# Folding a residual gate vector into the output weights of a transformer layer's merge stage

## The chip, the cores and the metric

The kernel runs on one core of one Trainium2 chip. The metric is device time in microseconds (us) of one execution; the time of a kernel is the median of its runs. The core has five engines with a queue of instructions each. TensorE (PE) multiplies matrices out of SBUF into PSUM; VectorE (DVE), ScalarE (ACT) and GpSimd (POOL) do elementwise work; the queue of SyncE (SP) issues nearly all the DMAs. Within one queue the order is fixed at compile time: an instruction that waits for another engine holds up everything behind it in its own queue.

## The reference, cut to what matters

One layer over 2048 latent tokens of width 1024. The stage that matters merges two branches, projects the result with `w_out`, and adds it to the residual stream `x` under a per-channel gate `g1` that comes from the conditioning vector:

```python
def branch_merge(attn_o, gm_o, ga_logit, gb_logit, w_br_attn, w_br_gm, w_out):
    y = jax.nn.sigmoid(ga_logit) * (attn_o @ w_br_attn) + jax.nn.sigmoid(gb_logit) * (gm_o @ w_br_gm)
    return y @ w_out
...
x = x + g1 * branch_merge(attn_x, gm_x, ga_x, gb_x, w_br_attn[l], w_br_gm[l], w_out[l])
h2 = modulate(x, norm2_g[l], sh2, sc2)
x = x + g2 * sq_relu_mlp(h2, w_ff1[l], w_ff2[l])
```

`g1` has one value for each of the 1024 output channels, the same for all tokens. So `g1 * (y @ w_out)` equals `y @ (w_out * g1)`, with `g1` multiplied into the columns of `w_out`.

## The kernel before, in words

**Number format.** Every large product is computed from two parts of each operand. `split` (L150) makes them: ACT casts the operand to a high part (L153), and POOL or DVE subtracts that from the operand to get the low part (L157). `mm3` (L184) then issues three matmuls for one product: high by high (L186), high by low (L187), low by high (L188).

**The order of stages.** First the projections, then attention, then `merge` (L1402), then the feed-forward network (`ffn`, L1973). `merge` runs over 4 blocks `b` of 512 tokens. Each block has two phases.

*Branch phase*, 8 steps `m`, one for each 128 channels of `y`. A step's program order is:

1. SP issues the loads for step n + 2 (`load`, L1417): raw branch weights and gates.
2. `cast(n + 1)` (L1421): the branch weights of the next step are split, for branch "g" and then for branch "a". ACT casts; the low part is made by DVE for the first three steps of the kernel (n = 0, 1, 2) and by POOL after that.
3. 24 matmuls on PE: 12 for branch "g", 12 for branch "a", each group into a PSUM bank of its own. The first low-part weights are needed by the third matmul of the step.
4. DVE multiplies each bank with its gate (L1466, twice), adds the two (L1469); then `y` is split: ACT casts, DVE subtracts.
5. In block 0 only, one step of `load_w_out` (L1325): it fetches the next 128 rows of `w_out` and splits the present ones, 128x1024 elements; ACT casts, DVE subtracts. After the 8 steps the 8 pairs in `self.wo` stay in SBUF for all four blocks.

Block 0 has two extras. After step 2 the softmax sums of the last attention unit are multiplied on PE and copied out by ACT (L2369). After step 4 DVE takes their reciprocal (`inverse`, L2382), and SP waits for it.

*Output phase*, 4 tiles `tt` of 128 tokens with 2 halves of 512 channels each: 24 matmuls into one bank (`outer`, L1495), then a step of side work (preparing the inputs of the next block, or in block 3 the first operands of the feed-forward network, `h_first`, L1579), then the bank is multiplied with the gate vector `g1b` into a scratch tile `part` (L1518), and `part` is added to the tile of `x` (L1519). A finished tile is stored, and ACT sums its squares (`stored`, L1429) for the next normalisation.

`g1b` (128x1024, the gate in every partition, already halved for the form of the sigmoid that is used) is finished during attention, before `merge` begins.

**What sets the order.** `merge` puts its whole range of instructions into `self.pins`, and `order` (L2063) ties every pinned instruction to the one before it on its engine. In this stage, then, each engine runs in exactly the order in which the Python code emits. The feed-forward network is not pinned; a planner at compile time orders its instructions by the readiness it works out.

Of the kernel before, what the change touches and what calls it, by code (L numbers as in the profile page):

```python
# [13 lines left out]
ALU = mybir.AluOpType  # L14
# [58 lines left out]
class Kern:  # L73
# [1251 lines left out]
    def load_w_out(self):  # L1325
        nc = self.nc
        self.wo = []

        def fetch(k):
            st = self.sb("wo", [D])  # L1330
            nc.sync.dma_start(st, self.I["w_out"][0, k * P : (k + 1) * P, :])
            return st

        ahead = fetch(0)
        yield
        for k in range(KC):
            st = ahead
            if k + 1 < KC:
                ahead = fetch(k + 1)
            h, l = self.sb("wo", [D], F32R), self.sb("wo", [D], F32R)  # L1340
            self.split(st, h, l, lo_eng="dve")
            self.wo.append((h, l))
            yield
# [58 lines left out]
    def merge(self, first, start, last, ops, w1):  # L1402
        nc = self.nc
        for _ in start:
            pass
        self.close("mid", "base")
        self.open("early")
        self.open("late", side="right")
        for tag, shape in (("md", [TB]), ("js", [HK]), ("gt", [TB])):
            self.sb(tag, shape)  # L1410
        begin = self.here()
        steps = [(b, m) for b in range(NB) for m in range(KC)]
        raws, gts, ws = {}, {}, {}
        w_out = self.load_w_out()
        mod = self.mod_part(lambda: self.sb("md", [TB]), ("sh2", "sc2"), True)

        def load(n, tag="gt"):  # L1417
            raws[n] = self.br_raw(steps[n][1])
            gts[n] = self.gate_in(*steps[n], tag)

        def cast(n, lo_eng):  # L1421
            ws[n] = self.br_weights(raws.pop(n), lo_eng)

        def x_row(b, tt):
            xt = self.sb("xt", [D])
            nc.sync.dma_start(xt, self.x_block(b)[tt * P : (tt + 1) * P, :])
            return xt

        def stored(b, tt, xt):  # L1429
            nc.sync.dma_start(self.x1_d[b][tt * P : (tt + 1) * P, :], xt)  # L1430
            junk = self.sb("jk", [D], mybir.dt.bfloat16)
            col = b * TT + tt
            nc.scalar.activation(
                junk, xt, AF.Square, accum_out=self.ss2[:, col : col + 1]
            )

        load(0, "gx")
        load(1)
        cast(0, "dve")
        last.leave(self.sb("raw", [TB]))  # L1440
        next(w_out)
        inp = first
        for b in range(NB):
            y = []
            for m in range(KC):
                n = b * KC + m
                if n + 2 < len(steps):
                    load(n + 2)
                if n + 1 < len(steps):
                    cast(n + 1, "pool" if n > 1 else "dve")  # L1450
                w, gt = ws.pop(n), gts.pop(n)
                for nm in ("g", "a"):
                    ps = self.bank([TB])
                    wh, wl = w[nm]
                    if n:
                        for k in range(4):
                            h, l = inp[nm][k]
                            self.mm3(ps, wh[:, k, :], wl[:, k, :], h, l, k == 0, k == 3)
                    else:
                        mm = nc.tensor.matmul  # L1460
                        for k in range(4):
                            for j, x in enumerate(inp[nm][k]):
                                mm(ps, wh[:, k, :], x, start=(j, k) == (0, 0), stop=False)
                        for k in range(4):
                            mm(ps, wl[:, k, :], inp[nm][k][0], start=False, stop=k == 3)
                    nc.vector.scalar_tensor_tensor(  # L1466
                        out=gt[nm], in0=gt[nm], scalar=1.0, in1=ps, op0=ALU.add, op1=ALU.mult
                    )
                nc.vector.tensor_tensor(out=gt["a"], in0=gt["a"], in1=gt["g"], op=ALU.add)  # L1469
                yh, yl = self.sb("y", [TB], F32R), self.sb("y", [TB], F32R)  # L1470
                self.split(gt["a"], yh, yl, lo_eng="dve")
                y.append((yh, yl))
                if b == 0:
                    next(w_out, None)
                    if m == 2:
                        last.sums(self.sb("raw", [TB]))
                    if m == 4:
                        last.inverse()
            inp = {}
            if b + 1 < NB:  # L1480
                side = self.br_inputs(b + 1, inp)
            else:
                for _ in mod:
                    pass
                self.close("early")
                self.open("back")
                side = self.h_first(ops, w1)
            next(side)
            xt, done = x_row(b, 0), None
            for tt in range(TT):  # L1490
                tok = slice(tt * P, (tt + 1) * P)
                after = x_row(b, tt + 1) if tt + 1 < TT else None
                banks = [self.bank([512]) for _ in range(2)]

                def outer(n, ks):  # L1495
                    cs = slice(n * 512, (n + 1) * 512)
                    for k in ks:
                        self.mm3(
                            banks[n], y[k][0][:, tok], y[k][1][:, tok], self.wo[k][0][:, cs],
                            self.wo[k][1][:, cs], k == 0, k == KC - 1,  # L1500
                        )

                head = KC - 1 if tt == 0 else KC
                if tt == 0:
                    for n in range(2):
                        outer(n, range(head))
                for n in range(2):
                    cs = slice(n * 512, (n + 1) * 512)
                    ps = banks[n]
                    outer(n, range(head if tt == 0 else 0, KC))  # L1510
                    if n == 0 and done:
                        stored(*done)
                        done = None
                    if b + 1 < NB or (tt, n) < (TT - 1, 1):
                        next(side, None)
                    next(mod, None)
                    part = self.sb("jk", [512])
                    nc.vector.tensor_tensor(out=part, in0=ps, in1=self.g1b[:, cs], op=ALU.mult)  # L1518
                    nc.vector.tensor_tensor(out=xt[:, cs], in0=xt[:, cs], in1=part, op=ALU.add)  # L1519
                done, xt = (b, tt, xt), after  # L1520
            stored(*done)
            if b + 1 < NB:
                for _ in side:
                    pass
        self.pins.append(range(begin, self.here()))
        for _ in range(2):
            next(side)
        self.close("late")
        self.open("rest")
        return side  # L1530
# [898 lines left out]
```

## Time and profile before

| | us |
|---|---|
| median of 3 runs (3010.51 to 3011.63) | 3011.14 |
| the profiled execution, whole | 3009.05 |
| its span, first to last instruction | 3007.2 |
| PE busy | 2931.6 |
| DVE busy | 2062.5 |
| ACT busy | 1417.9 |
| POOL busy | 652.8 |

The merge stage runs from about 1383 us to 1748 us of the span. Busy time counts instructions that do work; an engine that waits for a semaphore is idle. In a list of instructions in order of time, the columns are: start, duration, engine, line of the kernel, operation, result and operands, how many in a row, and in brackets how long the engine stood idle before it and what it waited for. In such lists `PEld` is the loading of the stationary operand of a matmul, which goes on beside the matmul before it. Matmuls overlap: each lasts about 0.39 us in its row, and the next starts about 0.23 us after it.

### The profile page before, as it was taken

The numbers are of one execution on the slowest core, as the hardware profiler recorded it, in microseconds if no ns is written. First come the engines' busy times: TensorE is split into PE (matmuls) and PEld (weight loads), VectorE is DVE, ScalarE is ACT, GpSimd is POOL, SyncE is SP. The second block draws the span as 40 slices with busy tenths as digits, with TensorE's granted clock in tenths as the row PEclk, the third lists the DMA queues.
The fourth block names the chain that finished last, engine by engine and source line by source line (L and its number), as shares of the span: only waits on it lengthen the run. The fifth ranks groups of instructions, "written<-read, shape, count | busy, mean of one in ns | idle before, by whom it ended". The sixth has DMA issues, their size and how long they took to land. (4 is left out here: it accounts for less than half of the span.)

```text
span 3007.2 us, 37935 instructions
## 1 busy us (share of the span) xinstructions
PE 2931.6 (97%) x13325; PEld 2206.7 (73%) x13325; DVE 2062.5 (69%) x2983; ACT 1417.9 (47%) x2318; POOL 652.8 (22%) x470
## 2 busy tenths in 40 slices
PE   7899999989999999999999989999999999999999
PEld 5778788876555555556888878888887888888887
DVE  5866487765788888867555587776676766654555
ACT  5554865553544545444222354444454344444432
POOL 0000000001999899894211200000000000000000
PEclk9999999999999999999999999999999999999999
DMA  7587866774010010016776658888766544447564
GB/s 276 184 295 272 307 215 217 256 247 140 24 36 26 25 37 22 22 36 191 238 215 194 183 198 308 307 305 303 261 219 224 186 154 154 154 154 277 210 209 155
DMA packets 386175, 559.04 MB, mean 186 GB/s; under 512 B 38640, under 2 KB 192416, under 8 KB 385984
## 3 DMA queue, kind: packets, MB, share of 16 engines
q1 hardware_dynamic: 373616, 535.89, 53.7%
q10 hardware_dynamic: 12368, 20.73, 1.8%
q8 instruction: 105, 1.72, 0.2%
q14 instruction: 86, 0.70, 0.1%
HBM read 379.75 MB, written 176.69 MB: 185 GB/s over the span
## 5 line engine op out<-in xcount | busy, mean ns | idle before, releaser
L2251 DVE TENSOR_REDUCE ts<-b 128x1 f32<-128x512 f32 x512 | 313.0, 681 | 75.3 <-PE b L2240 75.2
L2336 POOL TENSOR_TENSOR ac<-ac,p 128x512 f32<-128x512 f32 x214 | 306.3, 1463 | 50.5 <-ACT p L2308 50.5
L1858 DVE TENSOR_TENSOR b<-b,b 128x1024 fp32r<-128x1024 f32 x170 | 200.7, 1220 | 135.7 <-ACT b L1857 135.4
L1857 ACT CAST b<-b 128x1024 fp32r<-128x1024 f32 x170 | 170.6, 1050 | 222.2 <-PE b L1744 100.1
L2308 ACT ACTIVATE p<-b 128x512 f32<-128x512 f32 x384 | 194.1, 627 | 168.6 <-PE b L2304 168.1
L1743 PE MATMUL b<-b,b 128*128 128x512 f32 x680 | 265.2, 390 | 2.8 <-DVE b L1858 2.7
L1742 PE MATMUL b<-b,b 128*128 128x512 f32 x680 | 266.0, 391 | 1.6 <-DVE f L1879 1.4
L1744 PE MATMUL b<-b,b 128*128 128x512 f32 x680 | 264.7, 389 | 0.0
L2336 POOL TENSOR_TENSOR ac<-p,p 128x512 f32<-128x512 f32 x32 | 52.4, 1656 | 746.0 <-DMA raw<-in_w_mod 741.3
L2336 POOL TENSOR_TENSOR ac<-ac,t 128x512 f32<-128x512 f32 x152 | 205.0, 1378 | 0.0
L2285 PE MATMUL b<-h,h 128*128 128x512 f32 x576 | 188.0, 406 | 3.9 <-ACT p L2308 2.2
L2316 PE MATMUL b<-p,h 128*64 128x512 f32 x768 | 186.5, 609 | 0.0
L2304 PE MATMUL b<-h,h 128*128 128x512 f32 x576 | 179.1, 392 | 0.0
L1743 PE MATMUL b<-hb,b 128*128 128x512 f32 x446 | 173.8, 390 | 0.0
L1752 DVE TENSOR_TENSOR f<-f,b 128x512 f32<-128x512 f32 x160 | 109.0, 682 | 78.6 <-issue 45.8
L1742 PE MATMUL b<-hb,b 128*128 128x512 f32 x415 | 162.0, 390 | 0.3 <-DVE f L1752 0.3
L1744 PE MATMUL b<-hb,b 128*128 128x512 f32 x415 | 161.3, 389 | 0.0
L2285 PEld LDWEIGHTS b<-h,h 128*128 128x128 f32 x576 | 104.1, 189 | 65.1 <-DVE ts L2251 26.0
L1743 PEld LDWEIGHTS b<-b,b 128*128 128x128 f32 x680 | 127.6, 188 | 31.4 <-DVE b L1858 4.7
L1742 PEld LDWEIGHTS b<-b,b 128*128 128x128 f32 x680 | 127.6, 188 | 29.5 <-ACT b L1857 2.3
L1744 PEld LDWEIGHTS b<-b,b 128*128 128x128 f32 x680 | 127.7, 188 | 26.4
L157 POOL TENSOR_TENSOR bw<-bw,bw 128x512 fp32r<-128x512 f32 x58 | 75.8, 1328 | 235.7 <-ACT bw L153 235.7
(436 smaller groups left out, 7207.0 us busy)
## 6 DMA issues: line engine op xcount, KB each, us to landing
ao_d<-f SPq DMA_DIRECT2D x224, 256.0 KB
f<-in_w_ff SPq DMA_DIRECT2D x48, 1024.0 KB
b<-ao_d SPq DMA_DIRECT2D x85, 512.0 KB
b<-w2o_d SPq DMA_DIRECT2D x85, 512.0 KB
w2o_d<-f SPq DMA_DIRECT2D x112, 256.0 KB
f<-in_w_in SPq DMA_DIRECT2D x38, 512.0 KB
f<-x_d SPq DMA_DIRECT2D x64, 256.0 KB
hb<-ao_d SPq DMA_DIRECT2D x54, 256.0 KB
```

The lines of the kernel that those rows point to most:

```text
L1742: mm(ps, wh, hh, start=start and k == 0, stop=False, skip_group_check=True)
L1743: mm(ps, wh, hl, start=False, stop=False, skip_group_check=True)
L1744: mm(ps, wl, hh, start=False, stop=k == len(w) - 1, skip_group_check=True)
L1752: nc.vector.tensor_tensor(out=out, in0=in0, in1=in1, op=op)
L1857: nc.scalar.copy(h, f32(l))
L1858: nc.vector.tensor_tensor(out=l, in0=f32(l), in1=f32(h), op=ALU.subtract)
L2251: nc.vector.tensor_reduce(out=self.mx[:, t, h, c : c + 1], in_=ps[h], axis=AX.X, op=ALU.max)
L2285: self.nc.tensor.matmul(self.pts[j][h], k.KA[c][self.kv][:, ks], self.qa[h], start=True, stop=False, skip_group_check=True,)
L2304: self.nc.tensor.matmul(s, k.KB[c][self.kv][:, ks], self.qb[h], start=False, stop=True, skip_group_check=True,)
L2308: self.nc.scalar.activation(pt[h], s, AF.Exp)
L2316: nc.tensor.matmul(self.o[h * HD : (h + 1) * HD, :], k.V[c][:, i, self.kv * HD : (self.kv + 1) * HD], pt[h], start=j == 0, stop=j == NKT - 1,)
L2336: nc.gpsimd.tensor_tensor(out=self.acc[e][:, h], in0=old[:, h], in1=pt[h], op=ALU.add)
```

## The change

The gate is multiplied into the rows of `w_out` once, as they are loaded and before they are split. The output phase then adds the bank to `x` directly.

```diff
@@ load_w_out @@
             h, l = self.sb("wo", [D], F32R), self.sb("wo", [D], F32R)
+            nc.vector.tensor_tensor(out=st, in0=st, in1=self.g1b, op=ALU.mult)
             self.split(st, h, l, lo_eng="dve")
             self.wo.append((h, l))
             yield
@@ merge, output phase @@
                     next(mod, None)
-                    part = self.sb("jk", [512])
-                    nc.vector.tensor_tensor(out=part, in0=ps, in1=self.g1b[:, cs], op=ALU.mult)
-                    nc.vector.tensor_tensor(out=xt[:, cs], in0=xt[:, cs], in1=part, op=ALU.add)
+                    nc.vector.tensor_tensor(out=xt[:, cs], in0=xt[:, cs], in1=ps, op=ALU.add)
                 done, xt = (b, tt, xt), after
```

## The prediction

> **What bounds the kernel now.** First the page (how much of the span each engine works), then the busy times by stretch, to see which engine the merge stage waits for. Columns of the second view: stretch, its length, then busy time and count for PE, PEld, DVE, ACT, POOL, then the granted PE clock, the DMA share and GB/s.
>
> ```profile
> PE 2931.6 (97%) x13325; PEld 2206.7 (73%) x13325; DVE 2062.5 (69%) x2983; ACT 1417.9 (47%) x2318; POOL 652.8 (22%) x470
> ...
> 1383.00:1431.00 48.00, 47.97 (x203) 36.60 (x200) 35.05 (x44) 20.71 (x32) 14.48 (x11) 1.00 0.79 247
> 1431.00:1467.00 36.00, 36.00 (x160) 29.78 (x160) 23.56 (x35) 9.22 (x16) 2.75 (x2) 1.00 0.80 271
> 1467.00:1700.00 233.00, 233.00 (x1028) 190.26 (x1027) 123.94 (x186) 58.64 (x105) 58.56 (x46) 1.00 0.64 192
> 1700.00:1748.00 48.00, 48.00 (x237) 40.36 (x236) 34.09 (x53) 16.89 (x28) 0.00 (x0) 1.00 0.61 187
> 1748.00:1772.00 24.00, 15.77 (x57) 11.60 (x56) 19.75 (x29) 15.85 (x26) 0.00 (x0) 0.79 0.43 143
> ```
>
> PE is busy for all of the merge stage (1383 to 1748 us) at a granted clock of 1.00. Only behind it, at the entry to the feed-forward network, is there a hole: 15.77 us of 24. So work taken off DVE in the merge stage is worth nothing unless it shortens that hole, and work put on another engine costs nothing until PE starts to wait for it.
>
> **What is removed.**
>
> ```profile
> L1518 DVE TENSOR_TENSOR jk<-b,g x32: 678/684/692, 1440.8 to 1748.2; 128x512 f32<-128x512 f32 x32
> L1519 DVE TENSOR_TENSOR xt<-xt,jk x32: 691/692/693, 1441.5 to 1748.9; 128x512 f32<-128x512 f32 x32
> ```
>
> 32 multiplies at 0.684 us are 21.9 us of DVE. The add stays and reads the bank itself; I give it the 0.69 us that both of these take, one with an input in PSUM and one without. A bank is held as long as before. All 32 lie in the output phases, where PE never waits: 21.9 us at a price of 0. The last of them (1748.20) is beside the hole:
>
> ```profile
> 1748.93 0.69 DVE L1519 TENSOR_TENSOR xt<-xt,jk 128x512 f32<-128x512 f32 x1
> 1749.98 1.05 ACT L1433 ACTIVATE jk<-xt 128x1024 bf16<-128x1024 f32 x1
> 1752.19 1.05 ACT L1690 CAST f<-f 128x1024 fp32r<-128x1024 f32 x1
> 1753.29 0.79 PE L1742 MATMUL b<-in,f 128*128 128x512 f32 x1 [3.38 <-ACT f L1690]
> 1764.95 0.51 PE L1742 MATMUL b<-in,b 128*128 128x512 f32 x1 [3.17 <-ACT in L1540]
> ```
>
> PE's first wait (3.38 us) ends with ACT's cast L1690, and ACT is busy with transposed tiles and the square L1433 right up to it. That square's input was ready at 1749.62, and ACT came to it at 1749.98: it did not wait for DVE. Its input 0.73 us earlier gives nothing by itself. The planner may order these unpinned instructions anew; bounds: the whole 3.38 us gained, as much lost. I take 0.
>
> **What is added, and where it stands.** Eight multiplies of 128x1024. No such multiply is in the trace; the nearest row is a DVE operation of that shape between two SBUF operands:
>
> ```profile
> 1752.94 1.22 DVE L1696 TENSOR_TENSOR b<-f 128x1024 f32<-128x1024 f32 x1
> ```
>
> 8 x 1.22 = 9.8 us of DVE, less than was removed. But they stand at the end of a branch step of block 0, ahead of the cast that ACT makes of the same tile, and all is pinned. Here is step 1, DVE and then ACT, and the start of two steps on PE:
>
> ```profile
> 1393.85 1.28 DVE L157 TENSOR_TENSOR bw<-bw,bw 128x512 fp32r<-128x512 f32 x2
> 1395.05 1.28 DVE L1466 SCALAR_TENSOR_TENSOR gt<-gt,b 128x512 f32<-128x512 f32 x2
> 1396.36 0.69 DVE L1469 TENSOR_TENSOR gt<-gt,gt 128x512 f32<-128x512 f32 x1
> 1397.74 0.69 DVE L157 TENSOR_TENSOR y<-gt,y 128x512 fp32r<-128x512 f32 x1 [0.69 <-ACT y L153]
> 1398.69 1.22 DVE L157 TENSOR_TENSOR wo<-wo,wo 128x1024 fp32r<-128x1024 f32 x1 [0.26 <-ACT wo L153]
> 1399.84 0.68 DVE L1466 SCALAR_TENSOR_TENSOR gt<-gt,b 128x512 f32<-128x512 f32 x1
> ...
> 1397.62 1.05 ACT L153 CAST wo<-wo 128x1024 fp32r<-128x1024 f32 x1
> 1398.57 1.14 ACT L153 CAST bw<-bw 128x512 fp32r<-128x512 f32 x2
> ...
> 1389.40 0.39 PE L186 MATMUL b<-in,bw 128*128 128x512 f32 x1
> 1395.00 0.39 PE L186 MATMUL b<-in,bw 128*128 128x512 f32 x1
> ```
>
> A step lasts 5.60 us on PE (1389.40 to 1395.00). On DVE, by starts: the gated pair to the add 1.31; add to y's subtraction 1.38; that to the `wo` subtraction 0.95; that to the next pair 1.15: 4.79 us, so DVE keeps up. It does because ACT casts `wo` (1397.62) while DVE still works on y.
>
> After the change ACT cannot. DVE: y's subtraction, 0.60 to the next start, multiply 1.22, handover 0.03; ACT's cast 1.05, handover 0.03; only then the subtraction. 0.60 + 1.22 + 0.03 + 1.05 + 0.03 = 2.93 in place of 0.95. **The DVE step becomes 4.79 + 1.98 = 6.77 us, longer than PE's 5.60.** DVE is idle through the cast, yet nothing behind it can pass. On ACT, the branch-weight casts (1398.57) stand behind the `wo` cast, on POOL their subtractions stand behind those, and PE's next step but one needs the result.
>
> Is there slack? POOL, DVE and PEld around step 5's weights, and the last such wait:
>
> ```profile
> 1411.58 3.02 POOL L157 TENSOR_TENSOR bw<-bw,bw 128x512 fp32r<-128x512 f32 x2 [2.80 <-ACT bw L153]
> ...
> 1410.96 1.23 DVE L157 TENSOR_TENSOR wo<-wo,wo 128x1024 fp32r<-128x1024 f32 x1 [0.26 <-ACT wo L153]
> 1413.93 1.22 DVE L1469 TENSOR_TENSOR gt<-gt,gt 128x512 f32<-128x512 f32 x1
> ...
> 1413.39 0.19 PEld L188 LDWEIGHTS b<-in,bw 128*128 128x128 f32 x1 [0.19 <-POOL bw L157]
> 1425.11 0.19 PEld L188 LDWEIGHTS b<-in,bw 128*128 128x128 f32 x1 [0.46 <-POOL bw L157]
> ```
>
> None: PE already waits a little for POOL. Low-part weights come 2.43 us after the start of the `wo` subtraction (1410.96 to 1413.39). DVE and POOL also hinder each other: the add took 1.22 here and 0.69 in step 1; it ended 0.55 after POOL did. So it effectively began 2.27 us after the subtraction's end (1412.19), waiting for POOL. In the new order the add is asked for 1.15 + 1.31 = 2.46 us after that subtraction's start, 1.23 after its end, and waits 2.27 - 1.23 = 1.04 us: a step of 7.8 us. The Trainium skill, "SBUF — State Buffer", section "SBUF: two separate sides", says that a VectorE operation with two SBUF inputs and a GpSimd operation that reads SBUF exclude each other for a whole instruction, whichever came first; these rows agree (1.22 against 0.69), and by that rule the sum below is 10.9, while two engines that did not hinder each other would make it 7.9.
>
> **The sum.** The `wo` subtractions of steps 0 to 5, until POOL has the weights for PE's step 7:
>
> ```profile
> 1391.76 0.69 DVE L157 TENSOR_TENSOR y<-gx,y 128x512 fp32r<-128x512 f32 x1 [0.74 <-ACT y L153]
> 1404.35 0.58 ACT L2369 COPY raw<-b 128x512 f32<-128x512 f32 x1
> 1417.93 0.93 DVE L2382 RECIPROCAL raw<-raw 32x128 f32<-32x128 f32 x1
> ```
>
> - Step 0: 1391.76 + 2.93 = 1394.69.
> - Step 1: 6.77 + 1.20 for DVE's own pair of weight subtractions (1393.85 to 1395.05) = 7.97.
> - Step 2: 7.8.
> - Step 3: ACT's copy L2369 delays POOL, so the add slips in between POOL's two operations and y's subtraction waits for the second one instead; about 7.5.
> - Step 4: 7.8.
> - Step 5: the reciprocal takes about 0.85 more, but most of it would have been spent waiting for POOL; 7.8.
>
> 1394.69 + 7.97 + 7.8 + 7.5 + 7.8 + 7.8 = 1433.56; plus 2.43 is 1435.99, where PE now has those weights at 1425.11. **PE reaches the output phase 10.9 us later.** Steps 6 and 7 of DVE run beside the output phase's first 42 matmuls, which need `wo[7]` only after them; at 0.23 us each that is 9.7 us of cover, and it is nearly used up, at a price of 0 that could become 1.
>
> Bounds: without any waiting between DVE and POOL, steps 2 to 4 take 6.77 and step 5 7.62, which gives 7.9 us; with a further 0.5 us in four steps, for y's subtraction also waiting, 12.9.
>
> DMAs: SP's fetch of the next rows comes later too, since it stands behind gates whose tiles DVE must free, and behind the reciprocal.
>
> ```profile
> 1421.30 0.42 SPq L1331 DMA_DIRECT2D wo<-in_w_out  x1
> 1428.19 1.05 ACT L153 CAST wo<-wo 128x1024 fp32r<-128x1024 f32 x1 [0.68 <-DMA wo<-in_w_out]
> ```
>
> That fetch takes 6.9 us to be of use. In the new order it goes out some 2.4 us after the reciprocal (about 1430), is there at 1437, and its multiply comes at about 1439: covered by 2 us. If that cover goes, DVE waits as long as it is late.
>
> **The profiled execution** took 3009.05 us, so it becomes 3009.05 + 10.9 = 3020.0; it lies 2.1 us below the median of the runs, to which the same 10.9 us is added: 3011.14 + 10.9 = **3022.0 us**.
>
> **The rivals.** Under 0.2% (6.0 us: 3005.1 to 3017.2) a measurement of this kernel can hardly tell from no change.
>
> *The clock drops in the new stalls.* PE would wait about 7.8 - 5.6 = 2.2 us in a step. The trace has lost clock behind 3.38 and 3.17 us (0.79 above) and behind less:
>
> ```profile
> 49.02 0.57 PE L1742 MATMUL a<-f,h 128*128 128x384 f32 x1 [2.27 <-ACT f L712]
> ...
> 49.00:54.00 5.00, 4.55 (x21) 4.13 (x21) 4.85 (x8) 3.46 (x6) 0.00 (x0) 0.66 0.83 264
> 600.00:700.00 100.00, 91.94 (x425) 72.71 (x425) 57.14 (x109) 52.68 (x89) 0.00 (x0) 1.00 0.75 240
> PE a L1742 <- ACT a L2176: 2.5, 2, 1.9
> ```
>
> It kept it behind a wait of 1.9 (the third row's stretch). A drop costs 5 x (1 - 0.66) = 1.7 us; in the steps a slower PE only waits less, so the last one alone counts: 3023.7. The Trainium skill, "TensorE: Matmul & The Clock Gate", Part 1 on the HAM clock gate, says that the clock halves after at least one idle window of about 3.4 us: by that rule no stall here is long enough, and the forecast stands. The rows at 2.27 and 3.17 us speak against so high a threshold.
>
> *Partly paid back.* The stall comes, but the planner's new order closes PE's first hole at the entry: 3022.0 - 3.4 = 3018.6; with the low bound of the stall 3015.6.
>
> *Hidden.* The multiply passes beside PE's work; it decides at a DVE step of 5.60 us. For it: PE has its weights ready a step ahead. Against it: 6.77, and PEld waiting already. 3011.
>
> *Faster.* No stall, and the entry's first hole closes, since the last add ends 0.73 us earlier and the planner moves L1690 ahead of the square: -3.4, and with the slow clock behind it another 2.6: 3005.1. It decides at ACT's order, which nothing above suggests will change.
>
> **How the numbers follow.** Forecast with its bounds (3019 to 3024) 0.60; clock 0.10; partly paid back 0.14; hidden 0.10; faster 0.04; above all of these 0.02. Above 3017.2: 0.60 + 0.10 + 0.02 + half of 0.14 = 0.79; faster 0.04; the rest 0.17. The range 3015 to 3026 holds the first two cases and most of the third.
>
> **What would show it.** Right: between 1395 and 1440 us PEld waits for POOL at L188 once a step, some 11 us in all; the `wo` subtractions on DVE follow each other by about 7.8 us; PE never waits in blocks 1 to 3; DVE's busy time falls by about 12 us. Wrong: steps of 5.6 us on PE in block 0, or a multiply that is not between y's subtraction and the cast.

## The result, and the profile after

The changed kernel takes 3028.12 us (median of 6 runs, 3026.55 to 3028.77), the kernel before 3013.56 us when all 6 of its runs are counted (3010.51 to 3017.51). The ratio is 1.0048 with a 95% interval of 1.0038 to 1.0059: the change makes the kernel slower by about 0.5%. The forecast was 3022.0 us with a range of 3015 to 3026: the direction holds, the time lies 2.1 us above the range. The six runs of the kernel before fall into two groups, three at 3010.51 to 3011.63 us, which the forecast had as its base, and three at 3015.49 to 3017.51 us.

Busy times by stretch in the changed kernel, the stretches chosen to match those shown of before (merge now begins at 1388.72 us; columns as there):

```profile
1388.00:1446.00 58.00, 50.63 (x200) 36.56 (x197) 41.75 (x49) 19.92 (x30) 15.09 (x10) 0.97 0.67 213
1446.00:1482.00 36.00, 36.00 (x160) 29.81 (x159) 23.10 (x31) 10.29 (x18) 3.08 (x2) 1.00 0.77 261
1482.00:1716.00 234.00, 234.00 (x1032) 191.13 (x1032) 111.75 (x168) 58.55 (x105) 58.51 (x46) 1.00 0.64 191
1716.00:1764.00 48.00, 48.00 (x239) 40.41 (x238) 29.41 (x46) 16.75 (x28) 0.00 (x0) 1.00 0.60 186
1764.00:1788.00 24.00, 15.86 (x61) 11.84 (x60) 20.08 (x29) 16.77 (x27) 0.00 (x0) 0.86 0.45 146
```

The first row is the new thing: PE is busy for 50.63 of 58 us in the branch steps of block 0; before, it was busy for 47.97 of 48 us there. In the next three rows DVE is busy for less than before (29.41 us against 34.09 in the last of them, for example) and PE does nothing it did not do before. The hole at the entry to the feed-forward network is as it was (15.86 of 24 us).

The same steps in order of time: DVE, then ACT, then the loads of PE's stationary operands that had to wait.

```profile
1399.73 1.22 DVE L157 TENSOR_TENSOR wo<-wo,wo 128x1024 fp32r<-128x1024 f32 x1 [1.11 <-ACT wo L153]
...
1404.76 0.69 DVE L157 TENSOR_TENSOR y<-gt,y 128x512 fp32r<-128x512 f32 x1 [0.69 <-ACT y L153]
1405.37 1.22 DVE L1341 TENSOR_TENSOR wo<-wo,g 128x1024 f32<-128x1024 f32 x1
1407.70 1.22 DVE L157 TENSOR_TENSOR wo<-wo,wo 128x1024 fp32r<-128x1024 f32 x1 [1.11 <-ACT wo L153]
1408.84 1.28 DVE L1467 SCALAR_TENSOR_TENSOR gt<-gt,b 128x512 f32<-128x512 f32 x2
1410.15 1.70 DVE L1470 TENSOR_TENSOR gt<-gt,gt 128x512 f32<-128x512 f32 x1
...
1415.47 1.23 DVE L157 TENSOR_TENSOR wo<-wo,wo 128x1024 fp32r<-128x1024 f32 x1 [1.11 <-ACT wo L153]
1422.99 1.23 DVE L157 TENSOR_TENSOR wo<-wo,wo 128x1024 fp32r<-128x1024 f32 x1 [1.11 <-ACT wo L153]
1430.79 1.23 DVE L157 TENSOR_TENSOR wo<-wo,wo 128x1024 fp32r<-128x1024 f32 x1 [1.11 <-ACT wo L153]
1438.57 1.22 DVE L157 TENSOR_TENSOR wo<-wo,wo 128x1024 fp32r<-128x1024 f32 x1 [1.11 <-ACT wo L153]
...
1406.62 1.05 ACT L153 CAST wo<-wo 128x1024 fp32r<-128x1024 f32 x1 [1.89 <-DVE wo L1341]
1407.57 1.14 ACT L153 CAST bw<-bw 128x512 fp32r<-128x512 f32 x2
...
1410.10 0.19 PEld L188 LDWEIGHTS b<-in,bw 128*128 128x128 f32 x1 [1.57 <-POOL bw L157]
1417.19 0.19 PEld L186 LDWEIGHTS b<-in,bw 128*128 128x128 f32 x1 [2.13 <-ACT bw L153]
1418.55 0.19 PEld L188 LDWEIGHTS b<-in,bw 128*128 128x128 f32 x1 [1.06 <-POOL bw L157]
1433.20 0.19 PEld L188 LDWEIGHTS b<-in,bw 128*128 128x128 f32 x1 [1.57 <-POOL bw L157]
1440.97 0.19 PEld L188 LDWEIGHTS b<-in,bw 128*128 128x128 f32 x1 [1.57 <-POOL bw L157]
```

The multiply (L1341) runs; ACT's cast, which used to run beside y's subtraction, starts when it ends (ACT is idle for 1.89 us before it); DVE waits 1.11 us for the cast; only then does it subtract. The `wo` subtractions start 7.97, 7.77, 7.52, 7.80 and 7.78 us apart. On ACT the branch-weight casts begin 2.8 us after y's subtraction does (1404.76 to 1407.57), where before the change it was 0.8 us (1397.74 to 1398.57), and PE waits for what comes of them.

Not the whole difference comes from there. The two profiled executions differ by 3028.16 - 3009.05 = 19.1 us. Cut at the first branch matmul and at the first and the last matmul of `wo`, the branch steps of block 0 are 10.85 us longer (46.64 to 57.49), the rest of the merge is the same (317.42 and 317.41), but the stages ahead of the merge are 5.0 us longer (1383.70 to 1388.72) and those behind it 3.0 us (1259.4 to 1262.4). In the two traces the order of instructions on PE, POOL and SP is the same, and on ACT and DVE too outside the lines that the change touches, apart from one swap on each: ACT's last square goes ahead of a transposed tile, and DVE's L1696 ahead of a subtraction. So there were two questions: is the 10.85 us what was worked out, and are the other 8 us of the change's making?

### The profile page after: what moved, and what is told of

It is laid out like the page before. It is cut to its first block, busy times and chain, and to the rows that moved or that the text cites. A ratio compares the mean times of both kernels' runs of the same rounds, so it can differ in the third digit from the quotient of the medians.

```text
span 3026.1 us, 37899 instructions
## 1 busy us (share of the span) xinstructions
PE 2942.6 (97%) x13325; PEld 2214.1 (73%) x13325; DVE 2052.5 (68%) x2959; ACT 1417.4 (47%) x2318; POOL 653.9 (22%) x470
```

## The experiments

Every run's profile is cut at the same marks; all times are us and differences of start times, so the last digit can be off by one. "Ratio" is against the kernel before on the same chip, with its 95% interval.

| kernel | merge begins | branch steps, block 0 | rest of merge | behind it | ratio |
|---|---|---|---|---|---|
| before, as predicted from | 1383.70 | 46.64 | 317.42 | 1259.4 | |
| before, three more profiles | 1396.86, 1390.59, 1385.74 | 46.67, 46.72, 46.79 | 317.41 to 317.42 | 1265.4, 1261.1, 1260.8 | 1.0007, 0.9999, 1.0001 |
| changed, first | 1388.72 | 57.49 | 317.41 | 1262.4 | 1.0048 (1.0038 to 1.0059) |
| changed, three more | 1387.58, 1388.21, 1385.45 | 59.39, 57.53, 57.55 | 317.41 to 317.42 | 1262.8, 1262.5, 1259.6 | 1.0056, 1.0038, 1.0033 |
| multiplies alone | 1388.08 | 57.53 | 317.39 | 1262.2 | 1.0052 (1.0040 to 1.0064) |
| removal alone | 1387.62 | 46.67 | 317.40 | 1258.1 | 1.0003 (0.9993 to 1.0013) |
| multiply one step ahead | 1391.17 | 47.87 | 317.39 | 1260.7 | 1.0009 (0.9998 to 1.0021) |
| multiply into a spare tile | 1390.52 | 53.95 | 317.39 | 1260.3 | 1.0034 (1.0025 to 1.0044) |
| no POOL in block 0 | 1388.76 | 53.84 | 317.41 | 1261.1 | 1.0027 (1.0017 to 1.0038) |
| branch casts first | 1389.20 | 58.46 | 318.54 | 1260.5 | 1.0055 (1.0043 to 1.0067) |

### The two kernels again

No edit: the kernel before and the changed one side by side on one chip, once in a first set and twice in a second set on another chip.

> The kernel before, once more, on the chip that also runs the other kernels of this set. Theory A (what the change costs is the round trip between DVE and ACT in block 0, 10.8 us; the rest of the 14.6 us between the two medians is a difference between the occasions on which they were timed and falls on both kernels): about 3016 us, with the first matmul of the merge stage near 1388.7 us of the span as in the changed kernel's profile, not 1383.7. Theory B (the change also lengthens stages that it doesn't touch): about 3011 us, merge from 1383.7.

> The changed kernel beside the kernel before. Theory A: 10.8 us more than the kernel before on this chip, a ratio of 1.0036. Theory B: 14 to 15 us more, 1.0048.

> The kernel before again, for the lengths of its stages. Theory A (the change acts in block 0 alone; the stages ahead of the merge and behind it scatter from execution to execution, in both kernels): merge stage 364.1 us to 0.1 us; its start anywhere between 1383 and 1397 us; the rest behind it 1258 to 1266 us. Theory B (the stages it doesn't touch are longer after the change): start near 1384, rest near 1259, both below those of the changed kernel.

> The changed kernel again. Theory A: branch steps of block 0 57.5 us, or 59.4 where the clock is also lost at the last step, against 46.7 before; start and rest in the same spread as the kernel before. Theory B: start and rest above those of the kernel before by some 4 us together.

> The kernel before once more. Theory A: merge stage 364.1 us, its start and what follows it anywhere in the spread seen so far (1383 to 1397, 1258 to 1266). Theory B: start near 1384 and rest near 1259 again.

> The changed kernel once more. Theory A: branch steps of block 0 57.5 or 59.4 us, start and rest in the spread of the kernel before. Theory B: start and rest together about 4 us above the kernel before.

The unchanged kernel ran between 3008.31 and 3028.20 us in 12 runs of one set, and its profiled execution of 3028.20 us has a merge stage as long as that of 3009.05 us: 46.67 + 317.41 against 46.64 + 317.42. The 19 us lie in the stages ahead (13.2) and behind (6.0). So in the first set neither theory's start of the merge (1388.7 or 1383.7) came out. The changed kernel's merge starts and tails lie inside that spread. Over four profiles of each kernel the merge begins at 1387.5 us on average after the change and at 1389.2 before it, and what follows it takes 1261.8 and 1261.7 us: no sign that the change lengthens the stages it does not touch. Its ratios on shared chips were 1.0056 (1.0044 to 1.0068), 1.0038 (1.0026 to 1.0051) and 1.0033 (1.0022 to 1.0044); 10.85 us would be 1.0036. The two of the second set agree with that (3026.87 and 3024.62 against 3015.21 us: 11.7 and 9.4 us more); the first two comparisons lie above it, the one of the first set (1.0056) above what either theory expected. Theory A explains the merge to 0.1 us in three profiles of four, and puts the rest down to scatter, which the kernel before shows as well; why the medians of two comparisons came out 3.7 and 6.8 us above the 10.85 is not settled by it. One part of it is visible: in one profile the branch steps took 59.39 us, and there the clock was lost at the last step. Six rows from that execution, stretches of 6 us:

```profile
1411.58:1417.58 6.00, 3.83 (x16) 2.46 (x14) 4.72 (x6) 2.76 (x5) 1.19 (x1) 0.96 0.86 258
1417.58:1423.58 6.00, 5.85 (x20) 4.71 (x21) 4.19 (x5) 2.71 (x4) 2.63 (x3) 0.75 0.53 183
...
1429.58:1435.58 6.00, 4.35 (x18) 2.90 (x17) 4.88 (x7) 2.03 (x4) 3.05 (x2) 1.00 0.32 95
1435.58:1441.58 6.00, 4.34 (x17) 2.91 (x16) 4.85 (x5) 2.09 (x3) 2.99 (x2) 0.96 1.01 325
1441.58:1447.58 6.00, 6.00 (x21) 4.73 (x21) 4.20 (x6) 2.71 (x4) 1.47 (x1) 0.76 1.08 369
1447.58:1453.58 6.00, 6.00 (x28) 4.93 (x27) 4.16 (x5) 1.92 (x3) 1.61 (x2) 1.00 1.04 395
```

The granted clock (third column from the end) falls twice. The first time is there in all four profiles of the changed kernel (from 1419.36, 1417.16, 1418.72 and 1416.26 us) and costs nothing that shows, since the next weights are late anyway. The second time no wait follows: 59.39 - 57.5 = 1.9 us.

### The two halves of the change

```diff
  (multiplies alone, in load_w_out; the output phase as before)
+            nc.vector.tensor_tensor(out=st, in0=st, in1=self.g1b, op=ALU.mult)
             self.split(st, h, l, lo_eng="dve")
```

> The eight multiplies alone are added; the output phase keeps its multiply and add, so the gate acts twice. Theory A: as the changed kernel, 10.8 us more than before, since the 32 multiplies removed were hidden; DVE's wo subtractions about 7.8 us apart. Rival (the removal gave something back, at the entry to the feed-forward network or in the output phases): clearly more than the changed kernel, by up to 6 us.

```diff
  (removal alone, in merge; load_w_out as before)
-                    nc.vector.tensor_tensor(out=part, in0=ps, in1=self.g1b[:, cs], op=ALU.mult)
-                    nc.vector.tensor_tensor(out=xt[:, cs], in0=xt[:, cs], in1=part, op=ALU.add)
+                    nc.vector.tensor_tensor(out=xt[:, cs], in0=xt[:, cs], in1=ps, op=ALU.add)
```

> Only the removal: no multiply at the load and none in the output phase, so the gate is left out. Theory A: within 1 us of before, because PE never waits in the output phases and the entry to the feed-forward network is set by ACT. Rival (21.9 us less of DVE is worth something): 2 us or more faster than before.

The multiplies alone bring the branch steps to 57.53 us, the changed kernel's length to 0.04; the removal alone leaves the merge at 46.67 + 317.40, the length of before to 0.01, and the time at a ratio of 1.0003 (0.9993 to 1.0013). All of the cost in the merge is in the eight multiplies, and 32 operations taken off DVE bought nothing that can be measured. The ratio of the multiplies alone, 1.0052, is above the 1.0036 of 10.85 us, as the changed kernel's is in the same set.

### What about the multiplies costs: their work or their place

```diff
  (multiply one step ahead: load_w_out hands out its step in two parts)
+            if k == 0:
+                scale(rows[0])
+            if k + 1 < KC:
+                scale(rows[k + 1])
+            yield
+            if k + 3 < KC:
+                rows.append(fetch(k + 3))
             h, l = self.sb("wo", [D], F32R), self.sb("wo", [D], F32R)
...
  (merge, block 0: the first part between the add and y's split)
                 nc.vector.tensor_tensor(out=gt["a"], in0=gt["a"], in1=gt["g"], op=ALU.add)
+                if b == 0:
+                    next(w_out)
```

> The change with each multiply one step earlier: rows k+1 are multiplied in step k between the add and y's subtraction, where DVE otherwise waits 0.69 us for ACT's cast of y, and rows are fetched three steps ahead. Theory (the cost is the round trip multiply, cast, subtract, one behind the other): a DVE step of 1.31 + 0.60 + 1.13 + 0.60 + 1.15 = 4.79 us, as before the change, and a time within 1 to 2 us of before. Rival (the cost is 8 x 1.22 us of work on DVE, wherever it stands): about 10 us more than before, as the changed kernel.

The same eight multiplies, and the branch steps take 47.87 us, 1.2 more than before and 9.6 less than in the changed kernel. So the same work costs little in another place. The rows are also fetched earlier here, but that is not what helps: in the changed kernel no multiply waited for its rows. From this kernel's DVE in order of time:

```profile
1398.41 2.35 DVE L1335 TENSOR_TENSOR wo<-wo,g 128x1024 f32<-128x1024 f32 x2
...
1409.73 1.70 DVE L1477 TENSOR_TENSOR gt<-gt,gt 128x512 f32<-128x512 f32 x1
1411.36 1.22 DVE L1335 TENSOR_TENSOR wo<-wo,g 128x1024 f32<-128x1024 f32 x1
1413.10 1.21 DVE L157 TENSOR_TENSOR wo<-wo,wo 128x1024 fp32r<-128x1024 f32 x1
```

Each subtraction now starts 1.74 us after its multiply of the next rows (1411.36 to 1413.10) without waiting for ACT. The first step has two multiplies, since nothing ran ahead of it; that is the likeliest place of the 1.2 us: DVE's first `wo` subtraction comes 10.12 us after the first branch matmul (1391.17 to 1401.29), where it was 9.01 before (1383.70 to 1392.71). The total came out at 1.0009 (0.9998 to 1.0021): it cannot be told from the kernel before, and it isn't faster than it.

```diff
  (multiply into a spare tile; nobody reads it)
+            spare = self.sb("wo", [D])
+            nc.vector.tensor_tensor(out=spare, in0=st, in1=self.g1b, op=ALU.mult)
             self.split(st, h, l, lo_eng="dve")
```

> The multiply stays where the change put it, but writes to a tile that nobody reads, so ACT's cast doesn't wait for it; the gate is left out of the result. Theory (round trip): the DVE step is 4.79 + 1.13 = 5.92 us, up to 6.6 where the add also waits for POOL; 1.6 to 4.4 us more than before. Rival (DVE's work alone): about 10 us more, as the changed kernel.

Measured 7.3 us in the branch steps: above the expected 1.6 to 4.4, below the 10.85 of the changed kernel. The subtraction no longer waits for ACT, but in some steps waits for POOL instead, and one wait was not in the sum at all:

```profile
1405.97 1.22 DVE L1342 TENSOR_TENSOR wo<-wo,g 128x1024 f32<-128x1024 f32 x1
1407.10 2.31 DVE L157 TENSOR_TENSOR wo<-wo,wo 128x1024 fp32r<-128x1024 f32 x1
...
1430.19 0.31 SPq L2383 DMA_DIRECT2D rs_d<-raw  x1
1430.54 0.43 SPq L1385 DMA_DIRECT2D bw<-in_w_br_attn  x1
1431.07 0.45 SPq L1385 DMA_DIRECT2D bw<-in_w_br_gm  x1
...
1435.67 1.14 ACT L153 CAST bw<-bw 128x512 fp32r<-128x512 f32 x2 [2.03 <-DMA bw<-in_w_br_gm]
...
1436.34 0.19 PEld L186 LDWEIGHTS b<-in,bw 128*128 128x128 f32 x1 [3.09 <-ACT bw L153]
...
1438.50:1444.50 6.00, 6.00 (x22) 4.75 (x21) 3.88 (x4) 2.53 (x4) 3.70 (x3) 0.74 1.06 352
```

The loads of the last branch weights stand on SP behind the reciprocal's result. DVE's lag moves the reciprocal, and with a shorter step after it the load is no longer covered: 2.03 us on ACT. And behind that stall the clock is lost (0.74 in the last row, columns as above) with no later wait to absorb it: 6 x (1 - 0.74) = 1.6 us of the 7.3, by estimate. Work of 1.13 us a step where DVE has 0.8 to spare costs something; that much of the rival is right.

### The waits between DVE and POOL

```diff
  (no POOL in block 0: the low part of the weights of steps 3 to 7 by ACT)
+            if lo_eng == "act":
+                self.nc.scalar.copy(wh, raw[nm])
+                self.nc.scalar.copy(wl, raw[nm])
```

> The change, but in block 0 the low part of the branch weights of steps 3 to 7 is a second cast by ACT and not a subtraction by POOL, which leaves the low part wrong for those steps. Theory (1 us of each 7.8 us step is DVE's add waiting for POOL's instruction to end): adds of 0.69 us, wo subtractions 6.77 us apart, about 6.5 us more than before in place of 10.8. Rival (DVE and POOL don't hold each other up; the long add has another cause): adds and steps as in the changed kernel, 7.8 us, about 10 us more.

Measured 7.2 us, near the expected 6.5. Every add is 0.69 us long, and the steps that nothing else disturbs are the round trip alone:

```profile
1407.74 1.23 DVE L157 TENSOR_TENSOR wo<-wo,wo 128x1024 fp32r<-128x1024 f32 x1 [1.11 <-ACT wo L153]
1410.19 0.69 DVE L1474 TENSOR_TENSOR gt<-gt,gt 128x512 f32<-128x512 f32 x1
...
1414.51 1.23 DVE L157 TENSOR_TENSOR wo<-wo,wo 128x1024 fp32r<-128x1024 f32 x1 [1.11 <-ACT wo L153]
1421.29 1.23 DVE L157 TENSOR_TENSOR wo<-wo,wo 128x1024 fp32r<-128x1024 f32 x1 [1.12 <-ACT wo L153]
```

6.77 and 6.78 us apart, where the changed kernel has 7.77 and 7.52. About 3.6 of the 10.85 us go with POOL, but not all of it is the two engines holding each other up. Over the five steps between the first and the sixth `wo` subtraction DVE gains 2.3 us (38.84 to 36.53); that is their price here, although one of the steps is longer than 6.77 because DVE waits 0.58 us for PE. The other 1.3 us lie between the last of these subtractions and the output phase, where ACT's cast takes the place of POOL's subtraction.

### Branch casts first

```diff
  (merge, block 0, ahead of the step of load_w_out)
                 if b == 0:
+                    if m > 0:
+                        cast(n + 2, "pool")
                     next(w_out, None)
```

> The change, with the branch weights of step m+2 cast in step m ahead of the wo rows, so that neither ACT's casts nor POOL's subtractions of them stand behind the multiply. Theory (DVE's own step is the limit, and the weights are only the way in which PE hears of it): PE no longer waits in the branch steps but waits for the last wo rows at the start of the output phase; 5 to 11 us more than before. Rival (what costs is only the weights' place behind the wo cast on ACT): within 1 to 2 us of before.

Neither came out. The branch steps took 58.46 us and the output phase 1.1 more: 12.9 us in all, above both expectations. PE still waited in the branch steps. POOL's subtractions now start ahead of the multiply and stretch it in three steps; in three later ones they stretch the `wo` subtraction (2.23 to 2.35 us):

```profile
1405.85 2.33 DVE L1341 TENSOR_TENSOR wo<-wo,g 128x1024 f32<-128x1024 f32 x1
...
1439.34 1.14 ACT L153 CAST bw<-bw 128x512 fp32r<-128x512 f32 x2 [1.73 <-DMA bw<-in_w_br_gm]
...
1440.01 0.19 PEld L186 LDWEIGHTS b<-in,bw 128*128 128x128 f32 x1 [3.09 <-ACT bw L153]
```

A multiply of 2.33 us in place of 1.22 moved the wait from the add to the multiply. PE's wait at the start of the output phase was expected and is there (0.8 us at L187, for `wo`), which says that DVE's lag counts. That PE waited in the branch steps as well was not foreseen; its longest wait there (at 1440.01) ends a chain that begins with a DMA, since ACT's cast waits 1.73 us for weights whose load stands behind the reciprocal, as in the kernel with the spare tile. The result speaks against the rival that the weights' place on ACT is all, but does not exclude it: the edit brought costs of its own.

## Why the forecast was right in its mechanism and wrong in its number

- **"21.9 us at a price of 0."** Right: removal alone left the merge at 364.07 us (46.67 + 317.40). The add from PSUM takes 0.69 us, as taken (rows of 677 to 690 ns).
- **The hole at the entry, 0.** Right for its first wait: 3.38 us in both profiles. So neither case with that hole closed came, and the 2.6 us that the case *Faster* adds stand there without a working.
- **"The DVE step becomes 6.77 us", and 7.8 with POOL.** Right, one by one: forecast 7.97, 7.8, 7.5, 7.8, 7.8; measured 7.97, 7.77, 7.52, 7.80, 7.78. Without POOL the step is 6.77 where nothing else adds to it.
- **"PE reaches the output phase 10.9 us later."** Measured 10.85 (57.49 - 46.64), and 10.7 to 10.9 in two more profiles. The cover of `wo[7]` held: no wait of PE in the output phases.
- **The clock.** The rival's price was 1.7 us at the last step alone; it happened in one of four profiles and cost 1.9. Behind the longest stall it happened in all four, where it was absorbed as worked out. It was weighed as a case of its own beside the forecast, but it comes on top of it in some executions.
- **What would show it.** PEld's waits were said to be at L188, for POOL. Of its 12.1 us in the first profile 5.8 are that, 5.3 are at L186, for ACT, and 1.0 are for DVE: the high part is late too, not the low part alone. And DVE's busy time fell by 10.0 us (2062.5 to 2052.5), not by 12; time spent waiting for POOL counts as busy, and that is at least part of it.
- **The step that failed** is the last one: "it lies 2.1 us below the median of the runs, to which the same 10.9 us is added: 3011.14 + 10.9". Three runs within 1.1 us of each other were taken for the kernel's time. With the three runs added that came with the result, the base is 3013.56 us: 2.4 of the 6.1 us by which the forecast missed, and enough to carry the top of the range from 3026 past the measured time. Later sets put the median of the kernel before at 3013.46, 3014.60 and 3015.21 us, with single runs from 3008.3 to 3028.2. From 3015.21 the same sum gives 3026.1, and the changed kernel beside it took 3026.87 and 3024.62. The range had a term for every cost and none for the base. The other 3.7 us are the difference itself, 14.6 us in the first comparison against 10.9. They do not lie in the branch steps (10.85). In the first pair of profiles, what goes beyond those (8 us) lies in the stages around the merge, which scatter by more than that in the kernel before. How much of them is scatter and how much the clock in executions without a profile stays open.

## What to carry to other kernels

Moving work from a place where it runs 32 times to one where it runs 8 times is no gain when the first place is hidden and the second is a chain between engines that thereby becomes longer than the bounding engine's step (here 6.77 us against 5.60): write out the step's starts on every engine before and after, and compare them with that length. If an operation has to go there, put it one turn ahead, into a wait that exists anyway, as the kernel with the multiply one step ahead does. And when a forecast is an absolute time, give the base a spread of its own; here single runs of the kernel before lay up to 19.9 us apart, more than the effect.

## What the hardware showed that was not expected

The clock of TensorE fell behind shorter waits than the 2.27 us that the prediction had seen. In the changed kernel's first profile PE's waits in block 0 add up to this, by line and releaser (then total, times and longest), with the stretch that lost the clock below it:

```profile
PE b L188 <- POOL bw L157: 4.0, 4, 1.1
PE b L186 <- ACT bw L153: 2.6, 4, 1.7
PE b L188 <- DVE bw L157: 0.6, 1, 0.6
```

```profile
1418.72:1424.72 6.00, 6.00 (x20) 4.72 (x21) 4.20 (x5) 2.71 (x4) 2.64 (x2) 0.72 0.55 178
```

No wait is longer than 1.7 us, yet the stretch after 1418.72 us runs at 0.72. It follows two waits in a row, at L186 and, two matmuls on, at L188. In the other profile above, two steps with the same pair of waits (PE idle 1.65 and 1.66 us of 6) came out differently: the clock held behind the first until 1441.05 us and was lost there, behind the second (0.76). Each loss in block 0 is 3.41 us at 0.50. Counted in stretches of that length, back from the second loss, the first step's two waits fall into two stretches and the second step's into one:

```profile
1427.40:1430.81 3.41, 2.90 (x13) 2.05 (x12) 2.29 (x3) 1.91 (x3) 0.27 (x1) 1.00 0.00 0
1430.81:1434.22 3.41, 2.26 (x10) 1.52 (x10) 3.29 (x5) 0.22 (x2) 2.78 (x2) 1.00 0.10 29
...
1437.64:1441.05 3.41, 1.75 (x7) 1.03 (x7) 3.25 (x4) 1.13 (x3) 2.67 (x2) 1.00 1.07 349
```

PE is busy for 1.39 to 1.75 of the 3.41 us ahead of each of the five losses, and for 2.26 and 2.90 in the two stretches behind which it kept the clock. So idling for about half of such a stretch goes with a loss; no run tests this by itself, and it does not cover every loss: at 735.26 us of the kernel before, the clock was lost with PE busy for 2.93 of the 3.41 us ahead, on matmuls of 64x256. The Trainium skill, "TensorE: Matmul & The Clock Gate", Part 1 on the HAM clock gate, says that the clock halves after an idle window of about 3.4 us and that the window is free-running and not reset when a kernel starts. The unequal outcome of equal waits agrees with a freely running window; the 1.7 us does not agree with one that must be idle throughout.

DVE and POOL wait for each other's whole instructions: adds of 0.69 us are 1.70 long beside POOL, subtractions of 1.22 are 2.31, multiplies of 1.22 are 2.33, and with POOL out of the stage all adds are 0.69 again. POOL's pairs of subtractions, 2.55 us at their shortest before the change, are 3.52 beside those multiplies. In a profile this looks like a slow instruction, not like a wait.
